# A two-layer hybrid decoder trunk: 32x32 merges, taps and running sums arranged differently on TensorE's array

## The chip, the cores and the metric

The kernel runs on one core of one Trainium2 chip. The metric is the device time of one execution in microseconds (us). The engines are named as the profile names them: PE (TensorE's matmuls), PEld (its weight loads), DVE (VectorE), ACT (ScalarE), POOL (GpSimd) and SP (SyncE, whose queue issues nearly all DMAs).

## What is computed

The reference is a decoder of two layers on 512 tokens of 1024 features, all in float32. Layer 0 mixes tokens with four gated DeltaNet heads and eight banded softmax heads, which share one input projection and one output projection; layer 1 mixes with S5, a diagonal state-space recurrence of 64 groups. Behind each mixer come cross-attention into 256 memory tokens and a SwiGLU feed-forward part (width 2816). Cut to what the change touches:

```python
# gated DeltaNet, chunks of c rows (the kernel uses chunks of 128)
g = cumsum(log_decay)                                  # running sums within a chunk
decay = exp(where(causal, g[:, None] - g[None, :], -inf))
lower = where(strict, (k * beta) @ k.T, 0) * decay     # strictly lower triangular
sol = triangular_solve(lower + eye, rhs)               # needs the inverse of (I + lower)
# S5: states by a complex recurrence, then y = Re(C @ states) + d_skip * u
```

## The kernel before

**How instructions get their order.** Every operation goes through a recorder (class `Order`). A greedy list scheduler, with an estimate of each operation's cost, fixes one static sequence for each engine before anything is issued; ready operations of a later stage are pulled ahead to fill gaps. An engine runs its sequence strictly in order and waits at each instruction for its operands. `together(cost, calls)` records a group of matmuls that stay adjacent on PE and hands the scheduler one cost for the group. All operations are issued by one helper, so in the profile every single operation has line L439 and every matmul of a group L437; one goes by tile names (`ps` a PSUM bank, `t` a 128x512 scratch tile, `big` a 128x2048 tile, `hi` and `lo` weights).

**Large products.** A weight is loaded by SP into `raw` (two buffers), ACT rounds it to `hi`, DVE computes `lo` = raw - hi, and PE adds three products of 512 columns for each 128-row step: hi with the high part of the activations, hi with the low part, and lo with the high part. `gemm_tok` does this for four token tiles in four PSUM banks, 24 products a bank.

**The DeltaNet heads** (`mixer0`). There are four chunks of 128 tokens and four heads. For each chunk the running sums of the log decay stand as columns in `gc`; `gB` holds the same sums along rows, repeated over the partitions, and `Ds` = exp of their difference. `LTs` holds the transposed strictly lower matrices. The inverse of (I + lower) is built in three steps. (1) DVE solves all 32x32 diagonal blocks at once in a chain of 31 steps, each a product and a subtraction, on 64 partitions (one block each); the result goes by SP through DRAM (`scr2`) and back as `Xc`, DVE spreads it into four block-diagonal tiles `Xm`, and PE transposes those into `TTs`. (2) Pairs of 32 are merged to 64. (3) Pairs of 64 are merged to 128. Then the recurrence over the chunks runs. Meanwhile PE has other work: the z projection and, behind it, the value projection of the banded heads (`Vt`, the `gemm_tok` on columns 3080 of `w_in`), which the scheduler pulls ahead around the merges. Its four lo parts are called here the first to the fourth.

**Taps** (`s5_tables`). While layer 0's feed-forward products run, filler work builds S5's tables in eight blocks. In each, eight matrix products (four q, each the sum of two n) give the "taps", 128 rows by 32 columns for each q.

Of the kernel before, what the change touches and what calls it, by code (L numbers as in the profile page):

```python
# [12 lines left out]
AF = mybir.ActivationFunctionType  # L13
OP = mybir.AluOpType
AX = mybir.AxisListType

P = 128
# [3 lines left out]
NT = S // P  # L21
# [439 lines left out]
class Trunk:  # L461
# [23 lines left out]
    def t2(self, dt=F32):  # L485
        return self.o.tile(self.tp, [P, 512], dt, self.nm("t2"), "t2", T2)
# [113 lines left out]
    def mixer0(self, fill):  # L600
        tc, nc, a = self.tc, self.nc, self.a
        V, A, G, T = self.o.V, self.o.A, self.o.G, self.o.T
        sb = self.cp
        t2, tiny = self.t2, self.tiny
        small = lambda w, name="s", dt=F32: sb.tile([P, w], dt, name=self.nm(name), bufs=1)
        w_in = a["hyb_w_in"][0]

        xTv, _, actf, actt = self.feat_view([self.big() for _ in range(4)])
# [14 lines left out]
        upper = small(P, "upper")  # L623
# [4 lines left out]
        ktok = self.big(F32).rearrange("p (t c) -> p t c", t=4)  # L628
        cb = self.big(F32)
        attm = cb[:, :1280]  # L630
        level = cb[:, 1280:1408]
        self.o.SP.dma_start(level, a["level"])
        self.o.SP.dma_start(attm, a["attmask"])
        convw = small(48, "convw")
        self.o.SP.dma_start(convw, a["conv_t"])
# [129 lines left out]
        for c in range(NT):  # L765
            gB = self.bank()
            Dc = Ds[:, c]
            for h in range(4):
                o = c * 4 + h
                T.matmul(gB[:, hsl(h)], gl[:, o:o + 1].to_broadcast([P, P]), upper, start=True, stop=True)  # L770
            for h in range(4):
                o = c * 4 + h
                V.scalar_tensor_tensor(Dc[:, hsl(h)], gB[:, hsl(h)], gc[:, o:o + 1], causal, op0=OP.subtract, op1=OP.min)
            A.activation(Dc, Dc, AF.Exp)
# [34 lines left out]
        TTs = four()  # L809
# [49 lines left out]
        for c in range(NT):  # L859
# [4 lines left out]
            tp = self.transposes(lambda h: Xm[:, hsl(h)], 4)  # L864
            A.activation(TTs[:, c], tp, AF.Copy)
            Xms.append(Xm)
        for c in range(NT):
            XT, Xm = TTs[:, c], Xms[c]
            E = t2()
            V.tensor_tensor(h4(E), h4(LTs[:, c]), bc4(level), op=OP.mult)  # L870
            yp = self.bank()
            for h in range(4):
                T.matmul(yp[:, hsl(h)], E[:, hsl(h)], Xm[:, hsl(h)], start=True, stop=True)
            Y = t2()
            A.activation(Y, yp, AF.Copy)
            xp = self.bank()
            for h in range(4):
                T.matmul(xp[:, hsl(h)], XT[:, hsl(h)], Y[:, hsl(h)], start=True, stop=True)
            xtp = self.bank()
            for h in range(4):  # L880
                T.matmul(xtp[:, hsl(h)], Y[:, hsl(h)], XT[:, hsl(h)], start=True, stop=True)
            V.tensor_tensor(Xm, Xm, xp, op=OP.subtract)
            V.tensor_tensor(XT, XT, xtp, op=OP.subtract)
        lo_, up_ = slice(0, 64), slice(64, P)
        for c in range(NT):
            LT, XT, Xm = (h4(x) for x in (LTs[:, c], TTs[:, c], Xms[c]))
# [440 lines left out]
    def s5_tables(self):  # L1327
# [74 lines left out]
        for b in range(8):  # L1402
# [61 lines left out]
            for n in range(2):  # L1464
                V.tensor_tensor(cbv[:, n], C[n][:, qs, None, :].to_broadcast([P, 4, 2, 16]),
                                self.gmask[:, n, None, :, None].to_broadcast([P, 4, 2, 16]), op=OP.mult)
            tp = self.bank()
            for q in range(4):
                for n in range(2):
                    T.matmul(tp[:, q * 32:(q + 1) * 32], st[n][:, q * P:(q + 1) * P],  # L1470
                             cb[:, n * P + q * 32:n * P + q * 32 + 32], start=(n == 0), stop=(n == 1))
            ts = self.t2()
            tsv = ts[:, :P].rearrange("p (q c) -> p q c", q=4)
            A.activation(ts[:, :P], tp[:, :P], AF.Copy)
            di = ts[:, P:2 * P].rearrange("p (q c) -> p q c", q=4)
            V.tensor_tensor(di[96:], self.ident[96:, None, 96:].to_broadcast([32, 4, 32]),
# [226 lines left out]
```

## Time and profile before

| | |
|---|---|
| runs (3) | median 1561.4 us, 1559.45 to 1561.63 |
| profiled execution | 1559.76 us, of which the span is 1557.9 us |
| PE busy | 1523.2 us (98%) |
| DVE, ACT busy | 989.4 us (64%), 555.2 us (36%) |
| DMA | 184.06 MB, mean 118 GB/s |

The rows of a timeline give start, duration and a run of like instructions; a matmul's duration covers its whole way through a pipelined array, so the durations of neighbours overlap, and what one costs is read from one start to the next. An idle time and what released it stand in brackets behind the instruction that waited. A float32 product that isn't split into hi and lo is two matmul instructions (x8 is four products); a product of hi or lo with 512 columns, and a transpose, is one.

### The profile page before, as it was taken

Reading aid. Unit: us, or ns where it says so; the run is one execution under the profiler, and the core shown is the slowest. Engines: PE = TensorE matmul, PEld = TensorE weight load, DVE = VectorE, ACT = ScalarE, POOL = GpSimd, SP = SyncE. Lnnn points to the kernel's source line nnn. Section 1 sums busy time; section 2 is a strip of 40 time slices with the busy share of each in tenths; the row PEclk is TensorE's granted clock in tenths of the full one; section 3 lists DMA queues with packets and bytes.
Section 4 is the critical chain, followed back from the end, with each engine's and each line's share of the span. In section 5 each row is a group of like instructions: output and inputs, shape, how many; then the busy total and the mean of one; then the engine's idle time right before and its main releaser. Section 6 shows DMA issues by size and latency. Waiting matters only on the chain.

```text
span 1557.9 us, 20944 instructions
## 1 busy us (share of the span) xinstructions
PE 1523.2 (98%) x8132; PEld 1285.8 (83%) x8132; DVE 989.4 (64%) x1890; ACT 555.2 (36%) x996; POOL 57.6 (4%) x97
## 2 busy tenths in 40 slices
PE   7999999999999999999999899999999999999998
PEld 5887878689888888888888798888888888888886
DVE  6989666675657788635853899648647444234436
ACT  6533436624432343323441243323422332122311
POOL 1000000010100000010000000000000000000000
PEclk9999999999999999999999999999999999999999
DMA  6423224135213454436572553333212433233322
GB/s 180 123 70 96 82 81 136 60 99 154 81 62 115 122 187 143 172 117 196 196 234 86 213 174 136 115 114 103 75 55 82 122 96 95 82 108 105 98 68 95
DMA packets 125539, 184.06 MB, mean 118 GB/s; under 512 B 14144, under 2 KB 84800, under 8 KB 121344
## 3 DMA queue, kind: packets, MB, share of 16 engines
q1 hardware_dynamic: 125440, 182.73, 37.3%
q8 instruction: 64, 1.05, 0.3%
q14 instruction: 35, 0.29, 0.1%
HBM read 162.52 MB, written 20.19 MB: 117 GB/s over the span
## 4 chain that ended last, share of the span: by engine, by line
PE 84%; DVE 10%; DMA 2%; ACT 2%; issue 1%; SPq 0%; POOL 0%; DVEq 0%; ACTq 0%; POOLq 0%
PE ps L439 83%; DVE t L439 5%; DVE big L439 2%; DVE lo L439 2%; PE ps L437 1%; DMA raw<-in_xo_w_dram 1%; ACT big L439 1%; DVE tiny L439 1%; ACT hi L439 1%; DMA big<-s5m 0%; ACT L439 0%; DMA t<-in_x_t_dram 0%; DMA raw<-in_xv_w_dram 0%; DMA raw<-in_hyb_w_in_dram 0%; DMA prm<-in_dn_a_log_dram 0%
## 5 line engine op out<-in xcount | busy, mean ns | idle before, releaser
L439 PE MATMUL ps<-big,hi 128*128 128x512 f32 (+1 forms) x2368 | 648.3, 360 | 6.0 <-ACT hi L439 4.5
L439 PE MATMUL ps<-hi,big 128*128 128x512 f32 x1728 | 547.8, 394 | 0.7 <-ACT big L439 0.4
L439 PEld LDWEIGHTS ps<-big,hi 128*128 128x128 f32 x2368 | 419.8, 189 | 69.8 <-ACT hi L439 5.0
L439 ACT ACTIVATE hi<-raw 128x1024 fp32r<-128x1024 f32 (+2 forms) x252 | 263.4, 1046 | 517.5 <-PE ps L439 341.9
L439 DVE TENSOR_TENSOR lo<-raw,hi 128x1024 fp32r<-128x1024 f32 (+2 forms) x252 | 303.5, 1205 | 226.2 <-ACT hi L439 223.9
L439 PE MATMUL ps<-big,lo 128*128 128x512 f32 (+1 forms) x1184 | 424.1, 360 | 2.4 <-DVE lo L439 2.4
L439 PEld LDWEIGHTS ps<-hi,big 128*128 128x128 f32 x1728 | 322.5, 188 | 66.1 <-DVE big L439 0.9
L439 PE MATMUL ps<-lo,big 128*128 128x512 f32 x864 | 339.1, 394 | 4.2 <-DVE lo L439 3.9
L439 PEld LDWEIGHTS ps<-big,lo 128*128 128x128 f32 x1184 | 223.8, 189 | 34.0 <-DVE lo L439 3.0
L439 PEld LDWEIGHTS ps<-lo,big 128*128 128x128 f32 x864 | 162.4, 188 | 39.3 <-DVE lo L439 6.6
L439 ACT ACTIVATE big<-ps 128x256 fp32r<-128x256 f32 (+2 forms) x188 | 89.6, 508 | 205.8 <-PE ps L439 196.9
L439 ACT ACTIVATE t<-ps 128x512 f32<-128x512 f32 (+4 forms) x133 | 66.7, 512 | 155.7 <-PE ps L439 151.3
L439 DVE TENSOR_TENSOR big<-ps,big 128x256 fp32r<-128x256 f32 (+1 forms) x152 | 77.5, 541 | 54.6 <-ACT big L439 52.6
L439 DVE SCALAR_TENSOR_TENSOR big<-big,ps 128x512 f32<-128x512 f32 x56 | 38.3, 684 | 93.8 <-PE ps L439 93.8
L439 DVE SCALAR_TENSOR_TENSOR t<-t,ps 128x512 f32<-128x512 f32 x72 | 48.9, 681 | 56.7 <-ACT t L439 51.7
L439 ACT ACTIVATE big<-t 32x128 f32<-32x128 f32 (+2 forms) x148 | 64.4, 455 | 32.4 <-DVE t L439 14.2
L439 DVE SCALAR_TENSOR_TENSOR big<-big,tiny,t 128x512 f32<-128x512 f32 x96 | 66.5, 744 | 0.0
L439 PE MATMUL ps<-ident,t 128*128 128x128 f32 x336 | 61.1, 276 | 4.7 <-ACT t L439 3.0
L439 POOL TENSOR_TENSOR tiny<-tiny,mhalf 128x1 f32<-128x1 f32 (+1 forms) x28 | 23.6, 846 | 965.8 <-DVE tiny L439 965.8
L439 PEld LDWEIGHTS ps<-ident,t 128*128 128x128 f32 x336 | 41.8, 141 | 16.4 <-issue 5.6
L439 PE MATMUL ps<-big,big 128*128 128x256 f32 (+2 forms) x328 | 55.2, 314 | 0.0
L439 DVE TENSOR_TENSOR big<-t,big 128x512 fp32r<-128x512 f32 (+1 forms) x68 | 44.0, 680 | 13.9 <-ACT big L439 13.7
(144 smaller groups left out, 994.4 us busy)
## 6 DMA issues: line engine op xcount, KB each, us to landing
raw<-in_ffn_wg_dram SPq DMA_DIRECT2D x44, 512.0 KB, 3.6
raw<-in_ffn_wu_dram SPq DMA_DIRECT2D x44, 512.0 KB, 3.7
raw<-in_ffn_wd_dram SPq DMA_DIRECT2D x44, 512.0 KB, 3.8
s5m<-big SPq DMA_DIRECT2D x16, 1024.0 KB, 4.5
big<-s5m SPq DMA_DIRECT2D x16, 1024.0 KB, 5.1
raw<-in_hyb_w_in_dram SPq DMA_DIRECT2D x26, 512.0 KB, 3.6
raw<-in_xk_w_dram SPq DMA_DIRECT2D x16, 512.0 KB, 4.8
raw<-in_xv_w_dram SPq DMA_DIRECT2D x16, 512.0 KB, 3.8
```

The lines of the kernel that those rows point to most:

```text
L437: op.inst = getattr(self.eng[e], f)(*a, **k)
L439: op.inst = getattr(self.eng[e], fn)(*args, **kw)
```

## The change

It has three parts.

1. *Running sums.* `gB` was 16 products of the repeated log decay with an upper triangular matrix; it becomes 16 transposes of the repeated columns of `gc`.
2. *The merge of 32s.* Before, each chunk had its matrix masked to the blocks at this level (`level`, loaded by a DMA, and a DVE product `E`), three times four full 128x128 products, an ACT copy and two DVE subtractions from whole tiles. After, only the 32x32 blocks that are needed are multiplied: 96 products of 32x32x32 in 48 groups of two, one in the upper and one in the lower half of the array's rows. All four chunks share one bank for each of the three steps (`yp`, `xtp`, `xp`). Two ACT copies of 32x512 make Y; the results are written to their places by two DVE operations of 32x16x32 and eight ACT copies of 32x4x32. The `level` load is gone.
3. *Taps.* The operands change places: the 32-column factor is held in the array and the 128 columns of the state are moved, each q in its own group of 32 columns of the array; the eight products of a block are one group. An ACT copy and a transpose bring the result back into the old layout.

```diff
-        level = cb[:, 1280:1408]
-        self.o.SP.dma_start(level, a["level"])
...
-                T.matmul(gB[:, hsl(h)], gl[:, o:o + 1].to_broadcast([P, P]), upper, start=True, stop=True)
+                T.transpose(gB[:, hsl(h)], gc[:, o:o + 1].to_broadcast([P, P]), self.ident)
...
-        for c in range(NT):
-            XT, Xm = TTs[:, c], Xms[c]
-            E = t2()
-            V.tensor_tensor(h4(E), h4(LTs[:, c]), bc4(level), op=OP.mult)
-            yp = self.bank()
-            for h in range(4):
-                T.matmul(yp[:, hsl(h)], E[:, hsl(h)], Xm[:, hsl(h)], start=True, stop=True)
-            Y = t2()
-            A.activation(Y, yp, AF.Copy)
-            xp = self.bank()
-            for h in range(4):
-                T.matmul(xp[:, hsl(h)], XT[:, hsl(h)], Y[:, hsl(h)], start=True, stop=True)
-            xtp = self.bank()
-            for h in range(4):
-                T.matmul(xtp[:, hsl(h)], Y[:, hsl(h)], XT[:, hsl(h)], start=True, stop=True)
-            V.tensor_tensor(Xm, Xm, xp, op=OP.subtract)
-            V.tensor_tensor(XT, XT, xtp, op=OP.subtract)
+        blk = [(slice(g * 64, g * 64 + 32), slice(g * 64 + 32, g * 64 + 64)) for g in range(2)]
+        all_ = [(c, h) for c in range(NT) for h in range(4)]
+        at32 = lambda x, c, h: x[:, (c * 4 + h) * 32:(c * 4 + h + 1) * 32]
...
+        def small(dst, rows, lhs, rhs):
...
+            for c, h in all_:
+                self.o.together(0.06, [((at32(dst, c, h)[rows[g]], lhs(c, h, g), rhs(c, h, g)), dict(start=True, stop=True))
+                                       for g in range(2)])
+        yp = self.bank()
+        small(yp, [b for _, b in blk], lambda c, h, g: LT4[c][blk[g][0], h, blk[g][1]],
+              lambda c, h, g: Xm4[c][blk[g][0], h, blk[g][0]])
+        Y = t2()
+        for _, b in blk:
+            A.activation(Y[b], yp[b], AF.Copy)
+        xtp = self.bank()
+        small(xtp, [a_ for a_, _ in blk], lambda c, h, g: at32(Y, c, h)[blk[g][1]],
+              lambda c, h, g: XT4[c][blk[g][1], h, blk[g][1]])
+        xp = self.bank()
+        small(xp, [b for _, b in blk], lambda c, h, g: XT4[c][blk[g][1], h, blk[g][1]],
+              lambda c, h, g: at32(Y, c, h)[blk[g][1]])
...
+        for a_, b in blk:
+            V.tensor_scalar(TT5[a_, :, :, b], v16(xtp)[a_], -1.0, None, op0=OP.mult)
+            for c in range(NT):
+                A.activation(Xm4[c][b, :, a_], v16(xp)[b, c], AF.Copy, scale=-1.0)
...
-            for q in range(4):
-                for n in range(2):
-                    T.matmul(tp[:, q * 32:(q + 1) * 32], st[n][:, q * P:(q + 1) * P],
-                             cb[:, n * P + q * 32:n * P + q * 32 + 32], start=(n == 0), stop=(n == 1))
+            self.o.together(0.5, [((tp[q * 32:(q + 1) * 32, :P], cb[:, n * P + q * 32:n * P + q * 32 + 32],
+                                    st[n][:, q * P:(q + 1) * P]), dict(start=(n == 0), stop=(n == 1)))
+                                  for n in range(2) for q in range(4)])
...
+            A.activation(ts[:, 2 * P:3 * P], tp[:, :P], AF.Copy)
+            tp = self.transposes(lambda k: ts[:, 2 * P:3 * P], 1)
             A.activation(ts[:, :P], tp[:, :P], AF.Copy)
```

The scheduler draws up its sequences anew, so the change also moves work that its lines don't mention. The instructions of the engines are otherwise the same ones, and their order differs only up to the end of the DeltaNet heads and in the stretch with the taps.

**DVE, inside the chain of 31 steps.** `big_119` is the block solve's X (its first run of each pair a product into `t2_184`, the second the subtraction); a shape of 64x135 or 64x252 tells how far the chain has come. `lo_346` is the value projection's first lo part, `lo_349` its second; `t2_252` is the `E` of the first chunk. Before:

```order
L439 TENSOR_TENSOR t2_184_260<-big_119_195 64x252
L439 SCALAR_TENSOR_TENSOR t2_189_265<-tiny_193_269,tiny_194_270 128x32
L439 TENSOR_TENSOR t2_252_328<-big_98_172,big_26_98 128x512
L439 TENSOR_TENSOR big_119_195<-big_119_195,t2_184_260 64x14x18
L439 TENSOR_TENSOR t2_189_265<-t2_189_265 128x32 x2
L439 TENSOR_TENSOR t2_184_260<-big_119_195 64x247
L439 TENSOR_SCALAR tiny_195_271<-t2_189_265 128x32
L439 TENSOR_TENSOR lo_346_422<-raw_344_420,hi_345_421 128x1024
L439 TENSOR_TENSOR big_119_195<-big_119_195,t2_184_260 64x13x19
```

Before, the first lo part is made in the early part of the chain, behind the product of 64x247; the second and the third follow later in the chain, and the fourth ahead of the spreading into `Xm`. After, the four are called `lo_330`, `lo_333`, `lo_336` and `lo_339`:

```order
L439 TENSOR_TENSOR big_119_195<-big_119_195,t2_184_260 64x6x26
L439 SCALAR_TENSOR_TENSOR big_68_142<-t2_242_318,normg_29_101 128x512
L439 TENSOR_TENSOR t2_184_260<-big_119_195 64x135
L439 TENSOR_TENSOR lo_330_406<-raw_328_404,hi_329_405 128x1024
L439 TENSOR_TENSOR big_119_195<-big_119_195,t2_184_260 64x5x27
L439 TENSOR_TENSOR lo_333_409<-raw_331_407,hi_332_408 128x1024
L439 TENSOR_TENSOR t2_184_260<-big_119_195 64x112
L439 TENSOR_TENSOR big_119_195<-big_119_195,t2_184_260 64x4x28
L439 TENSOR_TENSOR t2_184_260<-big_119_195 64x87
```

After, the first lo part stands behind the product of 64x135 instead of 64x247 (the solve's 27th step instead of its 19th), and the second right behind one more subtraction; the third and the fourth, and all that was `E`, no longer stand ahead of `Xm`.

**PE, from the value projection to the merge.** `ps_340` to `ps_343` are the banks of the value projection before, `big_9` an activation, `t2_244` to `t2_250` the four `Xm`, `big_98` is `LTs`. Before, the last products of the value projection ahead of the transposes of `Xm`, and the beginning of the merge:

```order
L439 MATMUL ps_343_419<-hi_351_427,big_8_79 128x512 x2
L439 MATMUL ps_343_419<-lo_352_428,big_8_79 128x512
L439 MATMUL ps_340_416<-lo_355_431,big_9_80 128x512
L439 MATMUL ps_340_416<-hi_354_430,big_9_80 128x512 x2
L439 MATMUL ps_245_321<-ident_1_72,t2_244_320 128x128 x4
L439 MATMUL ps_247_323<-ident_1_72,t2_246_322 128x128 x4
L439 MATMUL ps_253_329<-t2_244_320,t2_252_328 128x128
L439 MATMUL ps_249_325<-ident_1_72,t2_248_324 128x128 x4
L439 MATMUL ps_253_329<-t2_244_320,t2_252_328 128x128
L439 MATMUL ps_251_327<-ident_1_72,t2_250_326 128x128 x4
L439 MATMUL ps_253_329<-t2_244_320,t2_252_328 128x128 x2
```

Before, 77 products of the value projection stand ahead of the first transposes. After, with the banks called `ps_324` to `ps_327`, `ps_252` for `yp`, `ps_254` for `xtp` and `ps_255` for `xp`, `t2_253` for Y and `big_119` for `TTs`, the place reads (a count here is of products; a float32 product of `t` or `big` tiles becomes two instructions in the trace):

```order
L439 MATMUL ps_327_403<-lo_330_406,big_6_77 128x512
L439 MATMUL ps_327_403<-hi_329_405,big_6_77 128x512 x2
L439 MATMUL ps_327_403<-lo_330_406,big_6_77 128x512
L439 MATMUL ps_327_403<-hi_329_405,big_6_77 128x512
L439 MATMUL ps_245_321<-ident_1_72,t2_244_320 128x128 x4
L437 MATMUL ps_252_328<-t2_244_320,big_98_172 32x32 x2
L439 MATMUL ps_247_323<-ident_1_72,t2_246_322 128x128 x4
L437 MATMUL ps_252_328<-t2_244_320,big_98_172 32x32 x6
L439 MATMUL ps_249_325<-ident_1_72,t2_248_324 128x128 x4
L437 MATMUL ps_252_328<-t2_246_322,big_98_172 32x32 x6
L439 MATMUL ps_251_327<-ident_1_72,t2_250_326 128x128 x4
L437 MATMUL ps_252_328<-t2_246_322,big_98_172 32x32 x2
```

After, the transposes come when 45 products of the value projection have been issued, so 32 of them have moved behind; the first seven of these stand between `yp` and the 64 products on `ps_254` and `ps_255`, three more behind those.

**PE, in the stretch of the taps.** `ps_970` and (after) `ps_954` are the taps' banks of one block, the rows of 512 columns are products of the feed-forward part. Before:

```order
L439 MATMUL ps_970_1047<-t2_969_1046,t2_957_1034 128x32
L439 MATMUL ps_975_1052<-big_812_888,hi_986_1063 128x512 x2
L439 MATMUL ps_975_1052<-big_812_888,lo_987_1064 128x512
L439 MATMUL ps_974_1051<-big_813_889,hi_986_1063 128x512 x2
L439 MATMUL ps_970_1047<-t2_969_1046,t2_958_1035 128x32
L439 MATMUL ps_970_1047<-t2_969_1046,t2_957_1034 128x32
L439 MATMUL ps_970_1047<-t2_969_1046,t2_958_1035 128x32
L439 MATMUL ps_970_1047<-t2_969_1046,t2_957_1034 128x32
L439 MATMUL ps_970_1047<-t2_969_1046,t2_958_1035 128x32
L439 MATMUL ps_970_1047<-t2_969_1046,t2_957_1034 128x32
L439 MATMUL ps_970_1047<-t2_969_1046,t2_958_1035 128x32
L439 MATMUL ps_974_1051<-big_813_889,lo_987_1064 128x512
```

After, of another block, where nothing else has changed:

```order
L439 MATMUL ps_959_1036<-big_796_872,hi_971_1048 128x512
L437 MATMUL ps_954_1031<-t2_941_1018,t2_953_1030 32x128 x4
L437 MATMUL ps_954_1031<-t2_942_1019,t2_953_1030 32x128 x4
L439 MATMUL ps_959_1036<-big_796_872,hi_971_1048 128x512
L439 MATMUL ps_959_1036<-big_796_872,lo_972_1049 128x512
L439 MATMUL ps_960_1037<-big_796_872,hi_971_1048 128x512
L439 MATMUL ps_956_1033<-ident_1_72,t2_955_1032 128x128
L439 MATMUL ps_960_1037<-big_796_872,hi_971_1048 128x512
L439 MATMUL ps_960_1037<-big_796_872,lo_972_1049 128x512
```

Eight products, of which the scheduler had put some between products of 512 columns one by one, became one unbroken group, and one transpose (`ps_956`) was added behind its ACT copy.

## Rows read from the trace of the kernel before

**Rows 1.** The page's busy time of each engine, with share and instructions:
```profile
PE 1523.2 (98%) x8132; PEld 1285.8 (83%) x8132; DVE 989.4 (64%) x1890; ACT 555.2 (36%) x996; POOL 57.6 (4%) x97
```

**Rows 2.** Windows; stretch, length, busy us (instructions) by engine, TensorE clock, DMA share, GB/s:
```profile
106.00:145.50 39.50, 35.85 (x158) 28.69 (x157) 38.86 (x174) 10.51 (x17) 0.00 (x0) 1.00 0.23 64
...
175.00:241.00 66.00, 63.45 (x353) 53.01 (x352) 46.58 (x118) 28.87 (x63) 3.02 (x3) 1.00 0.36 112
...
460.00:700.00 240.00, 239.77 (x1220) 202.74 (x1219) 171.29 (x332) 86.05 (x149) 12.13 (x14) 1.00 0.44 142
```

**Rows 3.** Timeline of PE; start, length, operation, count [idle before <-releaser]:
```profile
123.38 1.29 PE L439 MATMUL ps<-hi,big 128*128 128x512 f32 x5
124.51 0.48 PE L439 MATMUL ps<-lo,big 128*128 128x512 f32 x1
...
133.37 0.50 PE L439 MATMUL ps<-lo,big 128*128 128x512 f32 x1 [3.12 <-DVE lo L439]
...
145.51 0.71 PE L439 MATMUL ps<-ident,t 128*128 128x128 f32 x5
```

**Rows 4.** Timeline of DVE, the block solve and what follows:
```profile
123.22 1.22 DVE L439 TENSOR_TENSOR lo<-raw,hi 128x1024 fp32r<-128x1024 f32 x1
...
133.74 0.23 DVE L439 TENSOR_TENSOR t<-big 64x135 f32<-64x135 f32 x1
...
144.34 2.48 DVE L439 TENSOR_TENSOR t<-t,masks 128x512 f32<-128x512 f32 x4
```

**Rows 5.** Timeline of SP, the store of the solved blocks:
```profile
137.50 0.48 SPq L439 DMA_DIRECT2D scr<-big  x1
```

**Rows 6.** Timeline of ACT, one hi part behind its load:
```profile
137.02 1.06 ACT L439 ACTIVATE hi<-raw 128x1024 fp32r<-128x1024 f32 x1 [7.49 <-DMA raw<-in_hyb_w_in_dram]
```

**Rows 7.** Windows of 3 us around a fall of the clock:
```profile
292.00:295.00 3.00, 1.55 (x8) 0.71 (x6) 3.00 (x12) 1.56 (x4) 0.00 (x0) 1.00 0.00 0
295.00:298.00 3.00, 2.60 (x8) 1.55 (x10) 0.89 (x4) 2.28 (x7) 0.00 (x0) 0.57 0.00 0
```

**Rows 8.** Groups of PE by form; count, busy us, mean ns, idle before:
```profile
L439 PE MATMUL ps<-upper,gl 128*128 128x128 f32 x32 | 4.1, 277 | 0.0
...
L439 PE MATMUL ps<-ident,rb 128*128 128x128 f32 x16 | 2.2, 272 | 0.0
```

**Rows 9.** Timeline of PE, the merges of 32s and of 64s:
```profile
154.14 1.06 PE L439 MATMUL ps<-big,t 128*128 128x128 f32 x8
155.03 1.06 PE L439 MATMUL ps<-t,t 128*128 128x128 f32 x8
...
156.41 0.22 PE L439 MATMUL ps<-t,big 64*64 64x64 f32 x1
156.42 0.22 PE L439 MATMUL ps<-big,t 64*64 64x64 f32 x1
156.47 0.22 PE L439 MATMUL ps<-t,big 64*64 64x64 f32 x1
```

**Rows 10.** Timeline of PE, groups of products in column halves:
```profile
268.61 0.51 PE L439 MATMUL ps<-hi,big 128*128 128x512 f32 x1
269.05 0.66 PE L437 MATMUL ps<-t,big 128*64 128x128 f32 x8
269.63 0.50 PE L439 MATMUL ps<-lo,big 128*128 128x512 f32 x1
...
300.12 1.09 PE L437 MATMUL ps<-t,big 128*64 128x128 f32 x16
301.14 0.66 PE L439 MATMUL ps<-ident,t 128*128 128x128 f32 x4
```

**Rows 11.** Timeline of PE, one block of the taps:
```profile
574.32 0.30 PE L439 MATMUL ps<-t,t 128*128 128x32 f32 x2
...
576.16 0.97 PE L439 MATMUL ps<-t,t 128*128 128x32 f32 x8
576.97 0.70 PE L439 MATMUL ps<-big,hi 128*128 128x512 f32 x2
```

More of the change, by code (lines that the diff above doesn't have):

```diff
@@ new lines, in mixer0 @@
+        all_ = [(c, h) for c in range(NT) for h in range(4)]
+        at32 = lambda x, c, h: x[:, (c * 4 + h) * 32:(c * 4 + h + 1) * 32]
+        LT4, XT4, Xm4 = ([h4(x[c]) for c in range(NT)] for x in ([LTs[:, c] for c in range(NT)], [TTs[:, c] for c in range(NT)], Xms))
+        def small(dst, rows, lhs, rhs):
+            for c, h in all_:
+                self.o.together(0.06, [((at32(dst, c, h)[rows[g]], lhs(c, h, g), rhs(c, h, g)), dict(start=True, stop=True))
+                                       for g in range(2)])
@@ L884, in mixer0 @@
+        v16 = lambda x: x.rearrange("p (c h k) -> p c h k", c=4, h=4)
+        TT5 = TTs.rearrange("p c (h i) -> p c h i", h=4)
+        for a_, b in blk:
+            V.tensor_scalar(TT5[a_, :, :, b], v16(xtp)[a_], -1.0, None, op0=OP.mult)
+            for c in range(NT):
+                A.activation(Xm4[c][b, :, a_], v16(xp)[b, c], AF.Copy, scale=-1.0)
         lo_, up_ = slice(0, 64), slice(64, P)
```

## The prediction

> **What bounds the kernel now.** First the busy times: PE works in 98% of the span, DVE in 64%, ACT in 36% [rows 1]. So a change counts where it shortens what PE issues, or moves a wait of PE. Next, three stretches of the windows. Between 460 and 700 us, where the first five blocks of the taps lie, PE is busy for 239.77 of 240.00 us: whatever leaves PE there leaves the span. Between 106 and 145.5 us, around the block solve, PE is idle for 39.50 - 35.85 = 3.65 us, while DVE is busy for 38.86 of 39.50 us: DVE sets the pace there. Behind that, from 175 to 241 us, PE has 2.55 us of idle time [rows 2]. Then the timeline of PE around the solve: at 124.51 us the first product with the value projection's first lo part starts without a wait; at 133.37 us PE has waited 3.12 us for the second lo part; at 145.51 us the first transposes of `Xm` come [rows 3]. DVE's timeline says why: the lo parts stand in one queue with the solve's 31 steps. The first lo part is made at 123.22 us, ahead of its use, and the product of 64x135, a late step, starts at 133.74 us [rows 4]. A wait of PE here is set by where the scheduler puts a lo part in DVE's queue.
>
> **Running sums.** 32 instructions busy for 4.1 us go; 16 transposes come, and 16 transposes of the same kind of repeated column are busy for 2.2 us [rows 8]: 1.9 us less. The transposes must now wait for the copy into `gc`; two products of 512 columns in between would hide a copy, and I price that at nothing. The saving brings PE to the next stage 1.9 us earlier, and is accounted for there.
>
> **The stage of the block solve.** Here the change isn't in its lines but in the order. The first lo part moves down DVE's queue, behind the product of 64x135. That product started at 133.74 us with two lo parts and one `E` ahead of it that are no longer there. A lo part takes some 1.15 us of DVE and `E` 0.6 (the first an estimate, the 1.22 us of its row less the overlap with the next; the second a quarter of the 2.48 us of the four operations of the same shape at 144.34 us), so the product ends at about 133.74 + 0.15 - 2.3 - 0.6 = 131.0, and the first lo part is ready at 132.2 us if DVE comes no earlier to this stage, and at 130.2 if it comes 2 us earlier, as PE does. PE wants it at 124.51 - 1.9 = 122.6 us and stands until 130.2 to 132.2: 7.6 to 9.6 us in one piece instead of 3.65 in all. Behind the waiting product stands all of PE. The second lo part comes 1.3 us behind the first, the third hi part some 3.7 us behind the end of the first lo part, when its raw buffer has been loaded again (before, ACT waited 7.49 us for such a load, and got on at 137.02 [rows 6]); the order has enough products in between for both. From the wait to the first transposes 41 products remain, at (124.51 - 123.38) / 5 = 0.226 us each [rows 3] 9.3 us, with what comes from small waits about 11: transposes at 141.2 to 143.2 us.
>
> The other condition of the transposes agrees with that. The solve's end moves up by the `E` and one lo part, 1.7 us; its store started at 137.50 us [rows 5], the first `Xm` at 144.34 us [rows 4], so 6.8 us go through DRAM, of which some may have been the fourth lo part, which stood ahead of `Xm` and no longer does. `Xm` is then there between 141.1 and 143.1 us.
>
> I take 142.2 us, 3.3 earlier than 145.51. But 77 - 45 = 32 products that stood ahead of the transposes now stand behind: 32 x 0.226 = 7.2 us. The stage costs 7.2 - 3.3 = 3.9, say **+4.0 us** (3 to 5), the running sums included. After a stretch of waits the clock can fall: between 295 and 298 us, behind a stretch in which PE was busy for 1.55 of 3 us, the granted clock is 0.57 [rows 7], which costs 3 x 0.43 = 1.3 us. If it happens here it lies in the slack between 41 products and the arrival of `Xm`, and I price it at nothing; without that slack it is 1.3 us.
>
> **The merge of 32s.** Eight instructions of 128 columns in a run take 155.03 - 154.14 = 0.89 us [rows 9]; twelve such runs, 10.7 us, go. There come 192 instructions of 32 columns, half in the upper and half in the lower rows of the array. No row shows this form. By columns one is a quarter of 0.89 / 8, 0.028 us. The merges of 64s show two halves side by side: an instruction of the one kind starts at 156.41 us, of the other at 156.42, of the first again at 156.47 [rows 9], so two in 0.055 to 0.06 us, what one of 64 columns costs by its columns. Fully side by side the merge is 96 x 0.028 = 2.7 us. If two in 0.055 is as fast as PE takes them, it is 5.3 us. About four changes to another shape come on top: eight instructions in column halves stand between two large products, and from 268.61 to 269.63 us, less one product, make 0.79 us, where four slots of 0.11 would be 0.44 [rows 10]; so up to 0.36 each, I take 0.3, 1.2 us. That gives -6.8 or -4.2 us. The row with two in 0.055 bounds from above only, as its instructions were twice as long; I take the middle, **-5.5 us**. A dearer bound: the eight 32-column instructions of the taps take 576.97 - 576.16 = 0.81 us, 0.10 each [rows 11], though with 128 columns of weights each, where the merge has 32; at 0.10 a pair the merge would gain 0.2 - 0.1, nothing.
>
> The four `E` and eight subtractions that leave DVE, and the copies that ACT does in their place (ten small ones for four of 512 columns), lie beside PE. All chunks now go through the three steps together: seven products stand behind `yp` (1.6 us) to cover the copies into Y, three (0.7 us) cover the copies ahead of the merge of 64s. A wait of some tenths can remain at each; on the other hand, the 32 products pushed back can fill part of the 2.55 us in which PE waits later. I set both off against each other: 0. The load of `level` was early and its absence changes nothing that waits.
>
> **The taps.** A block's sixteen instructions lie between 574.32 and 576.97 us, with four products of 512 columns in between: 2.65 - 4 x 0.226 = 1.74 us [rows 11]. After, they are one group of sixteen instructions of 128 columns, in four column groups. In two column groups sixteen such instructions take 301.14 - 300.12 = 1.02 us [rows 10], where one after another would be 16 x 0.11 = 1.78: two run side by side. Four side by side make four slots, 0.44, with 0.36 for the change of shape 0.80 us; the added transpose is 2.2 / 16 = 0.14 us [rows 8]. 1.74 - 0.80 - 0.14 = 0.80 for a block, **-6.4 us** for eight. The ACT copy and the longer way to the table lie beside PE, as this work runs far ahead of S5. Bounds: two side by side only, 0.88 + 0.36 + 0.14 = 1.38, -2.9 us; none, 1.78 + 0.36 + 0.14 = 2.28, +4.3 us.
>
> **The sum.** +4.0 - 5.5 - 6.4 = -7.9. The profiled execution took 1559.8 us, which gives 1551.9; the median of the runs lies 1.6 above it, 1553.5. I say **1553**.
>
> **Rivals.** Differences under 0.2% (3.1 us) can't be told from no change.
>
> (a) *The stall doesn't appear*: DVE comes to the first lo part much earlier, since it no longer has the masks' work and follows PE. Then the stage gives the running sums' 1.9 us back instead of costing 4.0: 1553 - 5.9 = 1547. Against it: DVE is busy for 98% of the stretch before [rows 2], and the steps of the solve themselves can't be shortened. 0.12.
>
> (b) *The halves of the merge take turns.* The two instructions of a pair write the same bank, as all chunks share one; the rows with two side by side don't say that theirs do. In turn, at 0.028 to 0.055 each, the merge takes 5.3 to 10.6 us and 1.2: -4.2 to +1.1, in the middle -1.6; 1553 + 3.9 = 1557. 0.13. The Trainium skill has a rule that speaks for it: "TensorEngine Tiling (Array Packing)", section Restrictions and Gotchas, Gotcha 1 (PSUM Pressure), says that different row tiles cannot access the same PSUM bank at the same time. No row of the trace before shows whether that holds here.
>
> (c) *Taps only two abreast*: +3.5, 1556.5. For it: no row has four. 0.08.
>
> (d) *A stall at the long end*: 9.6 us, with the clock falling and no slack to hide it: +1.0 + 1.3, and the transposes held back by the loads: 1555 to 1558. 0.06.
>
> (e) *Slower*: small instructions have a price of their own that doesn't shrink with their columns, and the halves take turns. Place: the three runs of the merge. At the 0.10 us of the taps' 32-column instructions 192 of them cost 19.2 + 1.2, +9.7 against the 10.7 of before, and the sum is +4.0 + 9.7 - 6.4 = +7.3: 1568. It decides from where the merge loses 5.5 us, at 0.078 us an instruction. Against it: instructions of 64 columns start every 0.055 us, and two halves beside each other. 0.06.
>
> **How the numbers follow.** My forecast has 0.55, with a range of its own of 1549 to 1556 (stage 3 to 5, merge -6.8 to -4.2, and 1.5 for what the runs differ by). (a) 0.12, (b) 0.13, (c) 0.08, (d) 0.06, (e) 0.06. The range leaves out (e) and half of (a): 1547 to 1559. Faster, below 1558.3: all of the forecast, (a) and (c), most of (b) and (d), 0.87; same 0.06, from the dear ends of (b) and (d); slower 0.07, (e) and a little for the unknown.
>
> **What would show it.** Stage: one wait of PE for a lo part of 7 to 10 us at about 122 us, the transposes of `Xm` near 142. Merge: the 128 instructions on `xtp` and `xp` in 1.8 to 3.5 us; 3.5 to 7 says (b), 10 or more (e). Taps: a run of 16 instructions in 0.5 to 0.8 us; 1.0 says (c). The prediction is wrong if PE finds the lo part ready, if PE waits between the steps of the merge for longer than the seven and three products, or if the pushed products meet an idle time later that they fill.

## The result

Beside each other on one chip the kernel before took 1560.5 us (median of 4 runs, 1559.45 to 1561.63), the changed kernel 1547.9 us (4 runs, 1546.71 to 1550.57): ratio 0.9917, 95% interval 0.9905 to 0.993, 12.6 us less. On another chip it took 1547.7 us against 1562.5 (ratio 0.9904, 0.9889 to 0.9919). That lies in the range of 1547 to 1559 that was predicted, 5 us under the forecast of 1553.

The page of the changed kernel, busy time of each engine:

```profile
PE 1507.4 (98%) x8220; PEld 1265.6 (82%) x8220; DVE 983.5 (64%) x1880; ACT 552.2 (36%) x1008; POOL 58.4 (4%) x97
```

PE is busy for 1523.2 - 1507.4 = 15.8 us less [rows 1]; its idle time, 1544.9 - 1507.4 = 37.5 us, is 2.8 us longer than before. The windows (columns as in [rows 2]) of the changed kernel, with the start of the program ahead:

```profile
0.00:46.00 46.00, 38.95 (x174) 29.36 (x175) 33.01 (x107) 26.89 (x53) 7.89 (x15) 1.00 0.60 171
...
106.00:145.50 39.50, 30.44 (x186) 24.34 (x185) 35.90 (x163) 11.45 (x19) 0.00 (x0) 0.87 0.18 44
...
175.00:241.00 66.00, 64.03 (x345) 52.57 (x345) 43.88 (x101) 28.79 (x60) 2.02 (x2) 1.00 0.40 130
...
460.00:700.00 240.00, 239.89 (x1246) 199.60 (x1245) 169.79 (x329) 86.17 (x154) 12.14 (x14) 1.00 0.46 151
```

Around the block solve PE now is idle for 9.06 us instead of 3.65, and the clock has fallen there to a mean of 0.87 [rows 2]; from 460 to 700 us PE is as full as before. The start has no row of before yet; it is this, so PE's idle time there went from 9.71 to 7.05 us:

```profile
0.00:46.00 46.00, 36.29 (x161) 27.21 (x162) 30.80 (x101) 30.12 (x55) 7.42 (x15) 1.00 0.60 170
```

PE's timeline of the changed kernel around the wait:

```profile
119.19 1.29 PE L439 MATMUL ps<-hi,big 128*128 128x512 f32 x5
129.54 0.79 PE L439 MATMUL ps<-lo,big 128*128 128x512 f32 x1 [9.06 <-DVE lo L439]
130.13 1.05 PE L439 MATMUL ps<-hi,big 128*128 128x512 f32 x2
130.99 0.63 PE L439 MATMUL ps<-lo,big 128*128 128x512 f32 x1
...
141.65 0.60 PE L439 MATMUL ps<-ident,t 128*128 128x128 f32 x4
```

The run of five products ahead of the first lo part starts at 119.19 us, 4.19 earlier than before [rows 3]. Then PE stands once, for 9.06 us, and the first transposes of `Xm` come at 141.65 us, 3.86 earlier than before. Behind the wait a pair of products takes 130.99 - 130.13 = 0.86 us, where it took 0.45. The clock says the same in windows of 4 us:

```profile
120.00:124.00 4.00, 0.48 (x3) 0.06 (x1) 2.96 (x19) 2.68 (x6) 0.00 (x0) 1.00 0.00 0
124.00:128.00 4.00, 0.00 (x0) 0.00 (x0) 4.00 (x17) 0.00 (x0) 0.00 (x0) 0.63 0.00 0
128.00:132.00 4.00, 2.46 (x6) 1.98 (x7) 3.86 (x10) 0.00 (x0) 0.00 (x0) 0.50 0.33 73
132.00:136.00 4.00, 4.00 (x13) 3.10 (x12) 3.90 (x36) 2.02 (x3) 0.00 (x0) 0.59 0.79 255
136.00:140.00 4.00, 4.00 (x19) 3.31 (x18) 3.46 (x30) 0.54 (x2) 0.00 (x0) 1.00 0.35 55
```

It is at half of its speed, 1.2 GHz, from within PE's wait until 6 us after its end. DVE's timeline shows the cause of the wait:

```profile
128.06 0.28 DVE L439 TENSOR_TENSOR t<-big 64x135 f32<-64x135 f32 x1
128.27 1.21 DVE L439 TENSOR_TENSOR lo<-raw,hi 128x1024 fp32r<-128x1024 f32 x1
...
138.78 0.68 DVE L439 TENSOR_TENSOR t<-t,masks 128x512 f32<-128x512 f32 x1
140.50 1.90 DVE L439 TENSOR_TENSOR t<-t,masks 128x512 f32<-128x512 f32 x3 [1.04 <-DMA t<-scr]
```

The first lo part is made at 128.27 us, right behind the product of 64x135; before, it was made at 123.22 [rows 4]. The first `Xm` follows at 138.78 us, the other three at 140.50, behind their load. The merge in the timeline of PE:

```profile
144.73 0.76 PE L437 MATMUL ps<-t,big 32*32 32x32 f32 x36
145.42 0.50 PE L439 MATMUL ps<-hi,big 128*128 128x512 f32 x1
145.75 0.40 PE L439 MATMUL ps<-lo,big 128*128 128x512 f32 x1
...
147.24 1.10 PE L437 MATMUL ps<-big,t 32*32 32x32 f32 x58
...
148.25 1.11 PE L437 MATMUL ps<-t,big 32*32 32x32 f32 x59
149.29 0.50 PE L439 MATMUL ps<-lo,big 128*128 128x512 f32 x1
```

The 128 instructions on `xtp` and `xp` take 149.29 - 147.24 = 2.05 us, 0.016 each. And one block of the taps:

```profile
568.01 0.27 PE L439 MATMUL ps<-ident,t 128*128 128x128 f32 x1
...
568.90 0.65 PE L437 MATMUL ps<-t,t 128*32 128x128 f32 x16
569.48 0.73 PE L439 MATMUL ps<-big,hi 128*128 128x512 f32 x2
```

Sixteen instructions take 569.48 - 568.90 = 0.58 us where the block had 1.74 [rows 11]; the added transpose at 568.01 costs little itself.

**Where the 13.0 us of the two profiled executions come from.** Outside the stretches that moved, PE's instructions are the same in both traces, so one can set the start of the same instruction after against before. The difference is -2.1 us at 47 us (the transposes that start at 47.64 and 45.55), -4.1 at 67 us, -4.2 at 119 us, -4.2 at 202 us (202.76 and 198.51), -4.7 at 241 us, -6.3 at 299 us, -5.5 at 369 us, -13.0 at 791 us (791.12 and 778.15) and at the end. So: the start 2.1 us, the running sums 2.0 (and 0.1 up to 119 us), then nothing from 119 to 202 us, where the long wait and the merge lie, 0.5 up to 241 us, 1.6 at 295 us, where the clock fell before [rows 7] and not after, 0.8 lost again by 369 us, and 7.5 from the taps. The nothing from 119 to 202 us is the sum of two stages, up to the transposes of `Xm` and from there. The windows between matched instructions, before:

```profile
119.52:145.51 25.99, 22.34 (x97) 17.47 (x96) 25.75 (x132) 8.71 (x14) 0.00 (x0) 1.00 0.32 82
145.51:202.76 57.25, 55.53 (x419) 49.12 (x417) 38.54 (x110) 25.84 (x69) 4.03 (x4) 1.00 0.27 83
```

and after:

```profile
115.33:141.65 26.32, 17.26 (x64) 13.63 (x63) 23.28 (x127) 7.86 (x13) 0.00 (x0) 0.81 0.24 61
141.65:198.51 56.86, 55.27 (x546) 46.91 (x545) 35.17 (x101) 27.60 (x77) 4.03 (x4) 1.00 0.29 94
```

### The profile page after: what moved, and what is told of

The parts are those of the page before. It is cut to its first block, busy times and chain, and to the rows that moved or that the text cites. A ratio compares the mean times of both kernels' runs of the same rounds, so it can differ in the third digit from the quotient of the medians.

```text
span 1544.9 us, 21109 instructions
## 1 busy us (share of the span) xinstructions
PE 1507.4 (98%) x8220; PEld 1265.6 (82%) x8220; DVE 983.5 (64%) x1880; ACT 552.2 (36%) x1008; POOL 58.4 (4%) x97
## 4 chain that ended last, share of the span: by engine, by line
PE 86%; DVE 8%; ACT 2%; DMA 2%; issue 1%; SPq 0%; POOL 0%; DVEq 0%; ACTq 0%; POOLq 0%
PE ps L439 84%; DVE t L439 5%; DVE big L439 2%; PE ps L437 2%; DVE lo L439 1%; ACT big L439 1%; ACT hi L439 1%; DVE tiny L439 0%; SPq L439 0%; DMA raw<-in_hyb_w_in_dram 0%; DMA raw<-in_xo_w_dram 0%; DMA raw<-in_xq_w_dram 0%; DMA t<-in_x_t_dram 0%; ACT L439 0%; DMA prm<-in_dn_a_log_dram 0%
## 5 line engine op out<-in xcount | busy, mean ns | idle before, releaser
L439 ACT ACTIVATE t<-ps 128x512 f32<-128x512 f32 (+6 forms) x147 | 68.5, 487 | 136.2 <-PE ps L439 127.2
L439 DVE TENSOR_TENSOR big<-t,big 128x512 fp32r<-128x512 f32 (+1 forms) x68 | 44.1, 679 | 12.1 <-ACT big L439 12.0
```

The source lines that it names most:

```text
L439: op.inst = getattr(self.eng[e], fn)(*args, **kw)
```

## The experiments

**The parts alone.** Three kernels with one part of the change each, all else as before. The running sums:

```diff
-                T.matmul(gB[:, hsl(h)], gl[:, o:o + 1].to_broadcast([P, P]), upper, start=True, stop=True)
+                T.transpose(gB[:, hsl(h)], gc[:, o:o + 1].to_broadcast([P, P]), self.ident)
```

> The running sums alone, all else as before. First theory (the wait for the first lo part comes with this part, since the solve's steps and the lo parts change places in DVE's queue as soon as gB is made earlier): 2 us gained by 57 us, then one wait of PE of 7 to 10 us near 122 us, some 5 to 6 us lost by the first transposes of Xm, so 1563 to 1566 us. Rival (the wait comes with the merge's new order): no wait beyond the 3.65 us of before there, 1558 to 1559 us. The start up to 47 us is as before by both.

Measured: 1565.3 us against 1561.1, ratio 1.0023 (1.0011 to 1.0035): slower. The wait, from PE's timeline of this kernel:

```profile
134.22 0.79 PE L439 MATMUL ps<-lo,big 128*128 128x512 f32 x1 [9.90 <-DVE lo L439]
```

9.90 us, with neither merge nor taps changed: the first theory holds. The sums' part saves PE some 1.5 us here (its matched instructions come 1.2 us later than before at 48.82 us, where the clock had fallen in the start, and 0.4 earlier at 119 us) and brings the long wait with it.

The merge, without the load of `level`; of its hunk, which stands whole in the change above:

```diff
-        self.o.SP.dma_start(level, a["level"])
...
-            V.tensor_tensor(h4(E), h4(LTs[:, c]), bc4(level), op=OP.mult)
...
+                self.o.together(0.06, [((at32(dst, c, h)[rows[g]], lhs(c, h, g), rhs(c, h, g)), dict(start=True, stop=True))
```

> The merge of 32s alone, without the load of level; running sums and taps as before. First theory: the start gains 2.1 us as it did after the whole change, no wait of PE over 4 us near 122 us, the merge gains 6 to 7 us: 1551 to 1553 us, and less by 1.6 if the clock doesn't fall near 295 us. Rival (the wait for the lo part comes with the merge): a wait of 7 us or more near 122 us, 1556 to 1558 us.

Measured: 1552.7 us, ratio 0.9949 (0.9932 to 0.9966). The longest wait of PE near the solve:

```profile
132.97 0.80 PE L439 MATMUL ps<-lo,big 128*128 128x512 f32 x1 [5.44 <-DVE lo L439]
```

The time is the first theory's; the wait of 5.44 us lies between the two: the merge's new order lengthens it by 1.8 us over the 3.65 of before, the sums' part by more. PE's idle time up to 46 us is 7.33 us, as after the whole change (38.67 us busy of 46).

The taps, of whose hunk these lines are the core:

```diff
-                    T.matmul(tp[:, q * 32:(q + 1) * 32], st[n][:, q * P:(q + 1) * P],
+            self.o.together(0.5, [((tp[q * 32:(q + 1) * 32, :P], cb[:, n * P + q * 32:n * P + q * 32 + 32],
...
+            tp = self.transposes(lambda k: ts[:, 2 * P:3 * P], 1)
```

> The taps alone, all else as before. First theory (four column groups side by side, 0.93 us gained at each of eight blocks as the matched instructions of the two traces have it): 7.5 us, 1553 us, and everything up to 550 us as before. Rival (part of the gain at the taps came with other work): the forecast's 6.4 us or less, 1554 to 1557 us.

Measured: 1555.2 us, ratio 0.9958 (0.9943 to 0.9973), so 4.2 to 8.9 us of 1561; the interval holds both figures. The matched instructions tell more: from 555 to 791 us the difference to before goes from +1.4 to -5.2 us, 0.90 to 0.93 at each block but the first, as after the whole change, and with the first block, ahead of which it is +2.2 at 549 us, 7.4 us in all. That is the first theory's figure. The median lies only 5.9 us under that of before; in this profile the clock falls near 38 us, ahead of the taps, and near 885 us, behind them, and the matched instructions lose 1.6 and 2.8 us there. The profile of before has neither fall.

**The start.** One line that loads what nothing reads, put back into the changed kernel:

```diff
+        level = cb[:, 1280:1408]
+        self.o.SP.dma_start(level, a["level"])
         self.o.SP.dma_start(attm, a["attmask"])
```

> The changed kernel with the load of level kept, which nothing reads. First theory (the 64 KB load by itself changes the order of the start: with it the order of PE up to 47 us is that of before): the 2.1 us at the start are gone, 1549.5 to 1550.5 us, and the wait near 120 us stands. Rival (the start gained by the other parts, the load costs its own few tenths at most): 1548 us, and PE's idle time up to 46 us stays near 7 us instead of 9.7.

Measured: 1552.2 us, ratio 0.9938 (0.9918 to 0.9958). The window of the start, and the wait that it holds:

```profile
0.00:46.00 46.00, 35.83 (x153) 26.31 (x154) 28.87 (x97) 28.64 (x53) 7.35 (x15) 0.96 0.59 170
```

```profile
37.75 0.88 PE L439 MATMUL ps<-ident,big 128*128 128x128 f32 x4 [2.82 <-DVE big L439]
```

PE is idle for 46 - 35.83 = 10.17 us again, and the 2.82 us wait for DVE ahead of four transposes is back; in the trace of before it is 2.82 us as well, at 37.36 us, and in that of the changed kernel there is none. All four kernels with the load (before, sums alone, taps alone, this one) are idle for 8.7 to 10.2 us up to 46 us, and all ten runs without it for 5.8 to 7.3. So the load, though only 64 KB, is worth some 2 us at the start. Without it the scheduler orders SP (the attention masks' load takes its place), DVE and PE differently; with it PE's sequence up to there is that of before, row for row. That it costs its order and not its own time is likely but not separated: SP issues it in 0.33 us, and the weight load that SP issues at 16.12 us before comes at 17.40 in the changed kernel, so no earlier without it. Which of the moved instructions ends the wait wasn't separated either. The mechanism is the first theory's, the time 1.7 us above its range. By the ratios, 0.9938 against 0.9917 and 0.9904 of the changed kernel, 3 to 5 us are lost; the clock in the profiled execution is also lower (mean 0.993 against 0.996, and 0.96 in the window of the start) and the intervals overlap, so only the start's share is shown.

**Halves of the array in the merge.** The pairs are taken from one half instead of both, all upper ones first; and, in another kernel, each half has its own bank:

```diff
-            for c, h in all_:
-                self.o.together(0.06, [((at32(dst, c, h)[rows[g]], lhs(c, h, g), rhs(c, h, g)), dict(start=True, stop=True))
-                                       for g in range(2)])
+            for g in range(2):
+                for (c, h), (d, k) in zip(all_[::2], all_[1::2]):
+                    self.o.together(0.06, [((at32(dst, x, y)[rows[g]], lhs(x, y, g), rhs(x, y, g)), dict(start=True, stop=True))
+                                           for x, y in ((c, h), (d, k))])
```

> The changed kernel with each step's products of the merge in another order: first all of the upper half of the array, then all of the lower, so that neighbours no longer lie in different halves. First theory (the halves run beside each other, a 32-column instruction by itself takes 0.028 to 0.032 us): the 128 instructions on xtp and xp take 3.6 to 4.1 us instead of 2.05. Rival (an instruction of 32 columns takes 0.016 us by itself, and nothing runs side by side): 2.05 us as in the changed kernel.

Measured: one run, 1557.5 us. The same place of the timeline:

```profile
147.80 2.01 PE L437 MATMUL ps<-big,t 32*32 32x32 f32 x61
149.62 0.21 PE L437 MATMUL ps<-t,big 32*32 32x32 f32 x1
...
149.74 2.38 PE L437 MATMUL ps<-t,big 32*32 32x32 f32 x61
152.05 0.80 PE L439 MATMUL ps<-hi,big 128*128 128x512 f32 x1
```

The first 61 instructions take 149.62 - 147.80 = 1.82 us, 0.030 each and nearly twice the 0.016 of the changed kernel: the halves do run beside each other. Then the clock falls, and the other 61 take still longer:

```profile
148.00:152.00 4.00, 4.00 (x128) 3.99 (x124) 1.37 (x2) 0.00 (x0) 0.00 (x0) 0.88 0.19 69
152.00:156.00 4.00, 4.00 (x28) 3.20 (x26) 0.00 (x0) 2.71 (x10) 0.00 (x0) 0.50 0.00 0
...
160.00:164.00 4.00, 4.00 (x24) 3.69 (x23) 0.91 (x3) 0.57 (x1) 0.00 (x0) 0.50 0.39 124
164.00:168.00 4.00, 4.00 (x30) 3.78 (x29) 0.00 (x0) 1.59 (x6) 0.00 (x0) 0.91 0.00 0
```

PE was busy all the time, with 32-column instructions for 4 us of it. The lost share of the clock from 148 to 168 us, times the length, is 6.8 us (the window left out has 0.50): that fall, and not the merge's own 2 us, makes most of what this run takes longer than the changed kernel.

```diff
-                self.o.together(0.06, [((at32(dst, c, h)[rows[g]], lhs(c, h, g), rhs(c, h, g)), dict(start=True, stop=True))
+                self.o.together(0.06, [((at32(dst[g], c, h)[rows[g]], lhs(c, h, g), rhs(c, h, g)), dict(start=True, stop=True))
...
-        yp = self.bank()
+        yp = [self.bank() for _ in range(2)]
```

> The changed kernel with a bank of its own for each half of the array in the three steps of the merge. First theory (the halves run beside each other though they write one bank): the 128 instructions on xtp and xp take 2.0 to 2.1 us as in the changed kernel. Rival (sharing a bank costs part of it, as the page's rule on row tiles would have it): 1.8 us (64 pairs of 0.028) or less.

Measured: one run, 1548.1 us, and in PE's timeline:

```profile
146.75 1.11 PE L437 MATMUL ps<-big,t 32*32 32x32 f32 x58
...
148.80 0.50 PE L439 MATMUL ps<-lo,big 128*128 128x512 f32 x1
```

2.05 us, to the hundredth what it takes with one bank. Sharing a bank costs nothing here. The rule of the Trainium skill, "TensorEngine Tiling (Array Packing)", Restrictions and Gotchas, Gotcha 1 (PSUM Pressure), that different row tiles cannot access the same PSUM bank simultaneously, isn't seen in this case. The two products of a pair also write different partitions (0 to 31 and 64 to 95 for `xtp`, 32 to 63 and 96 to 127 for `xp`); two row tiles that write the same partitions of a bank were not tried.

**The order within a taps block.**

```diff
-                                  for n in range(2) for q in range(4)])
+                                  for q in range(4) for n in range(2)])
```

> The changed kernel with the eight products of a taps block in the order q outside, n inside, so that two neighbouring products lie in the same column group. First theory (PE starts its instructions in their order, so four run side by side only when four neighbours lie in four groups): a block's run of 16 takes 0.9 to 1.8 us instead of 0.57, and the kernel loses 2.5 us or more at the eight blocks. Rival (an instruction waits only for its own column group, whatever stands in front of it): 0.57 to 0.6 us, no loss.

Measured: one run, 1549.3 us. One block:

```profile
570.18 0.66 PE L437 MATMUL ps<-t,t 128*32 128x128 f32 x16
570.78 0.73 PE L439 MATMUL ps<-big,hi 128*128 128x512 f32 x2
```

0.60 us: my first theory falls, the rival holds. The four groups overlap also when neighbours share one.

**The wait.** The weights of the value projection are given an earlier place in the scheduler's list (the constant 200 becomes 600, and in a later kernel 400, for this projection alone):

```diff
-        bias, self.o.bias = self.o.bias, self.o.bias - AHEAD
+        bias, self.o.bias = self.o.bias, self.o.bias - self.ahead
...
+        self.ahead = 600
         self.gemm_tok(w_in, 0, KT, 3080, actt, NT,
                       lambda tt, ps: A.activation(Vt[:, tt], ps, AF.Copy), tail=TAIL)
+        self.ahead = AHEAD
```

> The changed kernel with the value projection's weights (load, hi, lo) given to the scheduler as if they stood 600 operations earlier instead of 200, so that the first two lo parts stand around the product of 64x247 in DVE's queue again and all four ahead of the solve's end. First theory (PE's 9 us wait is set by the place of the first lo part alone): the wait falls under 4 us, the time to 1542 to 1544 us. Rival (DVE has no slack there: four lo parts, 4.6 us, ahead of the solve's end instead of two put off Xm and the merge by what the wait gains): 1546 to 1549 us.

Measured: 1555.8 us (7 runs, 1546.42 to 1558.93), ratio 0.9951 (0.9934 to 0.9969): slower than the changed kernel, against both theories. The wait at 120 us is gone; the longest that is left ahead of 180 us, and the clock behind it:

```profile
150.11 0.31 PE L437 MATMUL ps<-t,big 32*32 32x32 f32 x8 [1.01 <-issue]
```

```profile
144.00:148.00 4.00, 3.81 (x93) 2.85 (x94) 0.57 (x4) 2.97 (x5) 0.00 (x0) 1.00 0.84 259
148.00:152.00 4.00, 2.99 (x84) 2.17 (x84) 1.37 (x2) 1.51 (x8) 0.00 (x0) 0.84 0.04 13
152.00:156.00 4.00, 4.00 (x21) 2.91 (x21) 1.22 (x1) 1.90 (x4) 0.00 (x0) 0.50 0.18 13
...
168.00:172.00 4.00, 4.00 (x18) 3.50 (x18) 0.42 (x1) 0.60 (x1) 0.00 (x0) 0.60 0.02 4
...
180.00:184.00 4.00, 2.00 (x13) 1.41 (x12) 2.21 (x6) 0.14 (x1) 0.00 (x0) 1.00 0.00 0
```

The clock falls in the merge, behind a wait of 1.01 us, and stays at half up to 171 us; the mean clock of the span is 0.986 to 0.991 in six runs, and 0.997 in the one of 1546.42 us, which lies in the rival's range. PE also waits more from 180 us on, where the products of the value projection are used up: it is busy for 2.00 of the 4 us from 180. So where the clock hardly fell, the kernel without the long wait took only 1.3 us less than the 1547.7 of the changed kernel, on another chip.

> The changed kernel with the value projection's weights given to the scheduler as if they stood 400 operations earlier: the first two lo parts come eleven instructions of DVE's queue earlier than in the changed kernel, and all four ahead of the solve's end. First theory (without a long wait the products that were pushed behind are used up early, the merge and what follows have fewer large products between small ones, and the clock falls there in most executions): PE waits 6 to 8 us near 125 us instead of 9, the clock falls between 148 and 170 us in the profile, 1550 to 1555 us. Rival (the fall in the run with the parts much earlier was chance): no fall of the clock there, 1545 to 1548 us.

Measured: 1545.3 us (4 runs), ratio 0.9892 (0.9877 to 0.9906). The rival holds for this kernel: in the window from 148 to 152 us the clock is at 1.00, and PE waits 5.58 us. Its reason, chance, doesn't fit the earlier kernel, where six of seven runs have the lower clock.

```profile
148.00:152.00 4.00, 4.00 (x137) 3.15 (x135) 1.86 (x3) 2.42 (x7) 0.00 (x0) 1.00 0.02 6
```

```profile
125.22 0.79 PE L439 MATMUL ps<-lo,big 128*128 128x512 f32 x1 [5.58 <-DVE lo L439]
```

3.5 us less wait gave 2.4 us less than the changed kernel's 1547.7 on the same chip; the intervals overlap.

**Without the turned sums.** In the changed kernel `gB` is made by the products again:

```diff
-                T.transpose(gB[:, hsl(h)], gc[:, o:o + 1].to_broadcast([P, P]), self.ident)
+                T.matmul(gB[:, hsl(h)], gl[:, o:o + 1].to_broadcast([P, P]), upper, start=True, stop=True)
```

> The changed kernel without its first part: merge and taps new, running sums by the products with the upper triangle as before. First theory (the turned sums cost what they cost alone, some 4 us, since they bring the long wait): 1543 to 1545 us. Rival (beside the new merge the sums' part costs nothing net: its 2 us are gained and the wait differs little, 5.4 us with the merge alone and 9.1 with all three): 1547 to 1549 us.

Measured: 1545.8 us, ratio 0.9893 (0.9878 to 0.9907); PE waits 5.45 us at 133.51 us. By its time nearer to the first theory. So both kernels ran again on one chip:

> The changed kernel once more, beside the following ones on one chip, to compare them directly and to see how much of its spread goes with the granted clock. Expected 1546 to 1551 us, the slower runs at the lower mean clocks, as in the runs of before (1561 us at 0.997, 1564 at 0.993).

Measured: 1547.7 us (4 runs, 1546.69 to 1548.3).

> Merge and taps new, running sums as before, once more beside the changed kernel. First theory (the turned sums cost more by PE's wait than their 2 us): 1.5 to 3 us faster than the changed kernel. Rival (the difference of 2 us between two sittings was that of the chips and of the clock): within 1 us of it.

Measured: 1546.4 us (4 runs, 1544.35 to 1549.01), ratio 0.9902 (0.9885 to 0.9918): 1.3 us apart from the changed kernel, within both intervals. The turned sums cost 3 to 4 us alone; beside the merge their cost, 1.3 us by these medians, isn't shown to differ from nothing. Neither this kernel nor the one with the lo parts somewhat earlier is shown to beat the changed one.

## Why the prediction was right, and where it was off

**The direction and the size** came from the two terms that were costed from rows: merge and taps. The sum was 5 us too high, by steps that erred both ways: between the profiles -7.9 was forecast and -13.0 measured, and the 5.1 between them are -2.1 at the start, +1.6 in the stage of the solve, -2.1 in the merge, -1.1 in the taps, -1.6 by chance and 0.2 in small pieces.

**The start.** The step "The load of `level` was early and its absence changes nothing that waits" failed. It is worth some 2 us, priced at nothing: the order of three engines hung on it, as the kernel that keeps the load shows.

**The running sums**: 1.9 us forecast, 2.0 measured between the matched instructions at 47 and 67 us.

**The wait** was forecast at 7.6 to 9.6 us and is 9.06; the transposes at 141.2 to 143.2 us came at 141.65. That is partly luck: the start's 2.1 us brought PE and DVE there earlier, the clock's fall held PE up by more than 2 us, and I had priced both at nothing. The wait's cause was named rightly (the first lo part behind the product of 64x135), as the two kernels with earlier lo parts show, where PE waits 5.58 us or not at all. Its origin was not: I took it to follow from the change as a whole, and most of it comes with the running sums' part (9.90 us with them alone, 5.44 with the merge alone). That the clock's fall is hidden by slack was wrong: PE's work from the wait to the transposes took 141.65 - 129.54 = 12.1 us where 41 products at full clock take 9.3, while the first `Xm` was ready at about 139.5 us and the second at about 141.1, behind a late load. Of the 2.8 us the slack hid some 0.7. Between 119 and the transposes the changed kernel needs 26.32 us against 25.99, with 32 products (7.2 us) fewer: the stage costs 7.5 us, not the 5.9 that 4.0 and the sums' 1.9 make.

**The merge** was mis-sized: -5.5 forecast. From the transposes to the same instruction at 202 us it takes 56.86 us against 57.25, with 7.2 us of pushed products more: -7.6 us. PE's idle time in it is nearly the same, 1.59 us against 1.72, so it is work that went. The bound of "fully side by side" was right, at 0.032 for a pair against my 0.028, and the changes of shape cost less than the 0.3 us I gave them: the product right behind 36 small ones takes 145.75 - 145.42 = 0.33 us, 0.10 more than the usual. Rivals (b) and (e) are refuted by 2.05 us for 128 instructions; (b) also by the kernel with two banks. The pushed products aren't lost, as I had said, and PE's idle time from 175 to 241 us, 1.97 us instead of 2.55, is a little shorter, which I had set at nothing. In the kernel with the earliest lo parts, where they stand ahead of the merge, the clock falls in it; whether for that reason isn't shown.

**The taps**: four groups side by side, as forecast; 0.58 us for a run instead of 0.80, so the 0.36 us for the change of shape was too dear, and -7.5 instead of -6.4 (the rows of one block would even make 1.74 - 0.58 - 0.14 = 1.02 us, of which 0.93 was measured). Rival (c) is refuted.

**What came by chance**: at 295 us the clock fell in the profiled execution of before and not in that of the changed kernel (1.6 us in the matched instructions), but it does so in another profile of the changed kernel (0.97 from 280 to 340 us). It is no part of the change. Near 880 us the clock falls in ten of the twelve experiments' profiles, and in neither of the two compared here.

**Rival (a)** said 1547, and 1547.9 was measured, but its mechanism didn't occur: the stall is there. The time was low for other reasons.

**Open**: why the clock falls in the merge in the kernels with the lo parts earliest and with the halves in turn, and not in the others. The first trace shows a wait of 1 us among small products there, the second a longer stretch of small ones without a wait; no run separates them. Nor is it shown why the scheduler puts the first lo part later in DVE's queue when the running sums come earlier; no run follows its choices.

## What to carry to other kernels

Where a list scheduler orders everything, a removed 64 KB load or a handful of cheaper instructions can move other stages by as much as the edit itself: compare the whole order, stage by stage, and ask of each moved piece which engine was waiting there. A wait that is taken away need not be a gain: its filler work can lack later, as from 180 us on in the kernel with the earliest lo parts. And price small tiles by the bound in which they run side by side, once a row shows two halves or two column groups beside each other.

## What was not expected of the hardware

Instructions of 32 columns start every 0.016 us when they alternate between the halves of the array, with one bank or two, and every 0.030 us within one half. Four column groups run side by side in either order of issue (16 instructions in 0.58 and 0.60 us). The granted clock falls not only in a wait (at half from within the 9 us wait to 6 us after it): in one kernel it fell while PE was busy without a pause, in a stretch of 32-column instructions, in another behind a wait of 1 us in such a stretch, and it stayed at half for 14 and 20 us. Runs of the same kernel go with it: before, 1558.7 to 1562.7 us at a mean clock of 0.997 and 1565.2 to 1566.1 us at 0.992.
